# Second MLP of an encoder trunk: the first hidden unit's weight operands prepared during the output projection

## The chip, the cores and the metric

The kernel runs on one core of one Trainium2 chip (trn2). The metric is the device time of one execution in microseconds (us), as the median of several runs. The engines are named as in the profile: PE (TensorE, matmuls; PEld are its weight loads), DVE (VectorE), ACT (ScalarE), POOL (GpSimd) and SP (SyncE, whose queue issues all the DMAs that matter here).

## The reference, cut to what matters

Two layers (`DEPTH = 2`) on one sequence of 1024 rows of 1024 float32 values. Layer 0 mixes tokens with pooling, layer 1 with differential attention; after each mixer stands a gated MLP with 2816 hidden columns.

```python
for i in range(DEPTH):
    hn = _rms_norm(h, mix_norm[i])
    y = _pool_mixer(...) if i == 0 else _diff_attention(...)   # the latter ends in  o @ w_o
    h = h + y
    h = h + _conv_ffn(_rms_norm(h, ffn_norm[i]), ffn_w_up[i], ffn_conv_w[i], ffn_conv_b[i], ffn_w_down[i])
return _rms_norm(h, final_norm)

def _rms_norm(x, gain, eps=1e-6):
    y = x * lax.rsqrt(jnp.mean(x * x, axis=-1, keepdims=True) + eps)
    return y * gain

def _conv_ffn(x, w_up, conv_w, conv_b, w_down):
    g, u = jnp.split(x @ w_up, 2, axis=-1)
    gc = conv_b + sum(conv_w[j] * gp[:, j:j + s] for j in range(3))     # gp: g padded by one row
    return (jax.nn.gelu(gc, approximate=False) * u) @ w_down
```

## The kernel before

Each float32 factor of a matmul is kept as two parts, `hi` (rounded to the matmul's format, float32r) and `lo` (what is left), and each product is three matmuls: hi·hi, lo·hi and hi·lo. The up projection of the MLP is done by a scheme of Strassen's kind: for a block of 128 hidden columns (a *unit*; there are 22) the weights form four quarters, `u1`, `u2` (the two halves of the contraction, of the `u` columns) and `g1`, `g2` (of the `g` columns). Seven products of 12 matmuls each replace eight. Their weight operands are numbered 1 to 7: 1 is `u1`, 2 is `u2`, 4 is `g2`, and the others are sums: 5 is `g1+g2`, 6 is `g1+g2-u1`, 7 is `u1-g1`, 3 is `u2` minus operand 6. The row side has operands `x[1]` to `x[7]` with the same numbers: `x[1]`, `x[2]` come from rows 0 to 511, the others from sums of the upper and the lower 512 rows. A unit runs its products in the order 1, 6, 2, 7, 5, 4, 3.

`prep(j)` makes the weight operands of unit j from two loaded tiles `raw` (`ru` and `rg`, 512 KB each, `load(j)`): `parts` copies to `hi` on ACT (L379) and takes `lo = src - hi` (L380), `s_tile` makes a sum (L394). For j > 0 the sums and the `lo` are on POOL. For j = 0 they are on DVE, but for the `lo` of operands 1 and 2, which are on POOL.

The place of the change is the seam between the attention's output projection and this second MLP, at 1377 to 1478 us. The projection runs over eight row tiles of 128 rows, in the order `ORDER = (0, 4, 1, 5, 2, 6, 3, 7)`. For each tile (`wo_rest`):

- PE adds up 2 groups of 12 matmuls (`wo_acc`, L1251);
- DVE adds them to the residual `hs` (L175), ACT squares with a running sum (L176);
- the norm's factor is a chain of six small instructions of one column: `ss` (L188), `ms`, ACT's root `rt` (L190), `rt` (L192), `rs_p`, `rs_q`, `rs_r` (L194, L196, L198), all but `rt` on DVE;
- ACT scales to `xs` (L292), and PE transposes it by eight small matmuls into two PSUM tiles `tp` (L299), of which only two exist (`ps_dn`, two buffers), so that the second four transposes of a tile wait until ACT has read the first half of the tile before;
- for tiles 0 to 3, DVE takes `tp` into `xf` (L309). For tiles 4 to 7, ACT multiplies the first half by the gain in four instructions (L331, `b12`) and DVE does the second half (L309, `b22`), and then `combine` makes the sums of the two row halves (`t3`, `b12`, `b11`, `b21`: L340, L341, L342, L344) and the parts of `x[6]`, `x[7]`, `x[5]`, `x[4]`, `x[3]` (`put`: ACT L304, then DVE or POOL L305).

The profile leaves buffer numbers out of names: `t3` reads `t`, both `b12` and `b22` read `b`, `b11` and `b21` are halves of `xf`, `x[1]`, `x[2]`, `x[5]`, `x[3]` lie in `hnT_hi`/`hnT_lo`, and `x[6]`, `x[7]`, `x[4]` in tiles `x_hi`/`x_lo`.

A helper, `each_with_lag(ORDER, wo_rest, early)`, runs the combine of a tile after the first part of the next one, and calls `early()` once, after tile 1; `early` steps the generator `mlp`, which issues the loads of unit 0 and the first part of its prep. Outside of two hand ordered stretches (units 1 to 21 and the down projection) a list scheduler puts each engine's instructions in order, by its own estimate of their times; the order on each engine is then fixed, and each engine runs its list strictly in that order.

Pools that matter: `raw` (four buffers of 4 KB per partition, also used for `xf`), `s` (four buffers of 4 KB, of which a sum uses 2 KB), `wc` (16 weight parts), `u2`, `cm` and `wd` (free until unit 0 or 1 writes them). `w_combos(q)`, called in units 1, 3, 5 and so on, loads a 1 MB piece of the down weights into `wd` and makes four sums on DVE (L442 to L448).

Of the kernel before, what the change touches and what calls it, by code (L numbers as in the profile page):

```python
# [20 lines left out]
P = 128  # L21
# [3 lines left out]
NF = DFF // P  # L25
NT = S // P
NK = D // P
ORDER = (0, 4, 1, 5, 2, 6, 3, 7)
PLAN = ("...saq.bS..c.p", "st.aS.m.q.fb....F.c..")
PLAN7 = (".as.b....S.pqc.", "tmsaSqcb..f......F..")  # L30
# [59 lines left out]
def trunk_kernel(  # L90
# [133 lines left out]
    class Arena:  # L224


        def __init__(self, name):
            self.name = name
            self.s = None
            self.es, self.es_x, self.es_r, self.es_s, self.es_w = (ExitStack() for _ in range(5))  # L230

        def open(self):
# [22 lines left out]
        def open_up(self):  # L255
            self.es_r.close()
            if self.s is None:
                self.s = pool(self.es_s, "s", bufs=4, side="right")
            self.g = pool(self.es_r, "g", bufs=3, side="right")
            self.u2 = pool(self.es_r, "u2", bufs=2, side="right")  # L260
            self.cm = pool(self.es_r, "cm", side="right")
            self.wd = pool(self.es_r, "wd", side="right")
# [24 lines left out]
    def norm_to_x(layer, tt, ar, h_t, ss):  # L287
        x, G = ar.x, nc.gpsimd
        r = rstd(ss)
        with tc.high_priority(offset=20 if layer else 0):  # L290
            xs = ar.tile("gc", [P, D], F32, "xs")
            A.mul(xs, h_t, r)  # L292
            nc.sync.dma_start(h_dram[3 * layer][tt], h_t)
            cs = slice((tt % 4) * P, (tt % 4 + 1) * P)
            pts = []
            for q in range(2):
                pt = ar.tile("ps_dn", [P, 4, P], F32, "tp")
                for k in range(4):
                    PE.transpose(pt[:, k], xs[:, (4 * q + k) * P:(4 * q + k + 1) * P], ident)  # L299
                pts.append(pt)  # L300

        def put(i, src, eng):
            hi, lo = x[i]
            A.copy(hi[:, :, cs], src)  # L304
            eng.tensor_tensor(lo[:, :, cs], src, f32(hi[:, :, cs]), ALU.subtract)  # L305

        def gained(q, dst):
            gk = gcol[:, 2 + layer, 4 * q:4 * q + 4].unsqueeze(2).broadcast_to([P, 4, P])
            V.tensor_tensor(dst, pts[q], gk, ALU.mult)  # L309
            return dst  # L310

        q0, q1 = slice(0, 4), slice(4, 8)
        if tt < 4:
            xf = ar.xf[tt] = ar.tile("raw", [P, NK, P], F32, "xf")
            gained(0, xf[:, q0])
            gained(1, xf[:, q1])

            def combine():
                with tc.high_priority(offset=50):
                    combine2()  # L320

            def combine2():
                put(1, xf[:, q0], (V if layer else G))
                put(2, xf[:, q1], G)
        else:
            xf = ar.xf.pop(tt - 4)
            b11, b21 = xf[:, q0], xf[:, q1]
            b12, b22 = (ar.tile("s", [P, 2, 512], F32, n)[:, 0].rearrange("p (k f) -> p k f", f=P) if layer else
                        ar.tile("wc", [P, 4, P], F32, n) for n in ("b12", "b22"))
            for k in range(4):  # L330
                A.mul(b12[:, k], pts[0][:, k], gcol[:, 2 + layer, k:k + 1])  # L331
            gained(1, b22)

            def combine():
                with tc.high_priority(offset=20 if layer else 0):
                    combine2()

            def combine2():
                t3 = ar.tile("u2", [P, 4, P], F32, "t3")
                V.tensor_tensor(t3, b22, b12, ALU.subtract)  # L340
                V.tensor_tensor(b12, b12, b11, ALU.subtract)  # L341
                V.tensor_tensor(b11, t3, b11, ALU.add)  # L342
                put(6, b11, V)
                V.tensor_tensor(b21, b21, b11, ALU.subtract)  # L344
                put(7, t3, G)
                put(5, b12, V)
                put(4, b21, G)
                put(3, b22, G)

        return combine  # L350
# [12 lines left out]
    def ffn(layer, ar, tail, extra=None):  # L363
        G = nc.gpsimd
        wup, wdn, cv = w_up[layer], w_down[layer], convp[layer]
        raws, ws = {}, {}

        def load(j):
            if j >= NF:
                return  # L370
            raws.setdefault(j, [])
            for off in (DFF, 0):
                r = ar.tile("g" if layer == j == 0 else "raw", [P, NK, P], F32, "raw")
                nc.sync.dma_start(r, wup[:, off + j * P:off + (j + 1) * P].rearrange("(k p) f -> p k f", p=P))
                raws[j].append(r)

        def parts(src, eng=G):
            hi, lo = (ar.tile("wc", [P, 4, P], F32R, n) for n in ("w_hi", "w_lo"))
            A.copy(hi, src)  # L379
            eng.tensor_tensor(lo, src, f32(hi), ALU.subtract)  # L380
            return hi, lo

        def prep(j):
            if j >= NF:
                return
            w = ws.setdefault(j, {})
            ru, rg = raws.pop(j)
            u1, u2, g1, g2 = ru[:, 0:4], ru[:, 4:8], rg[:, 0:4], rg[:, 4:8]

            eng = (V, G)[j > 0]  # L390

            def s_tile(a, b, op):
                t = ar.tile("s", [P, 2, 512], F32, "s")[:, 0].rearrange("p (k f) -> p k f", f=P)
                eng.tensor_tensor(t, a, b, op)  # L394
# [314 lines left out]
            return ends[2:]  # L709

        load(0)
        first = prep(0)
        next(first)
        if layer:
            next(first)
        yield
        load(1)
        for _ in first:
            pass
# [16 lines left out]
    ar = Arena("a")  # L736
# [651 lines left out]
            ss = add_halves(hs, accs)  # L1388
        return norm_to_x(1, tt, ar, hs, ss)

    each_with_lag(ORDER, wo_rest, lambda: next(mlp))


    fin = []
# [53 lines left out]
```

## Time and profile before

| what | value |
|---|---|
| median of 3 runs | 2084.54 us (2083.7 to 2086.34) |
| profiled execution | 2089.84 us, span 2088.0 us |
| busy: PE, PEld | 2003.6 us (96%), 1665.6 us (80%) |
| busy: DVE, ACT, POOL | 1560.6 us (75%), 1024.4 us (49%), 895.3 us (43%) |
| mean granted PE clock | 0.983 |
| chain that ended last | PE 59%, DVE 5%, ACT 2%, DMA 2% |

Busy time is the sum of an engine's instructions in the span. A wait in brackets in a row is the idle time of the engine just before that instruction, and what ended it. All stages but the seam and the two ends keep PE busy without a pause.

### The profile page before, as it was taken

Reading aid. Unit: us, or ns where it says so; the run is one execution under the profiler, and the core shown is the slowest. Engines: PE = TensorE matmul, PEld = TensorE weight load, DVE = VectorE, ACT = ScalarE, POOL = GpSimd, SP = SyncE. Lnnn points to the kernel's source line nnn. Section 1 sums busy time; section 2 is a strip of 40 time slices with the busy share of each in tenths; the row PEclk is TensorE's granted clock in tenths of the full one; section 3 lists DMA queues with packets and bytes.
Section 4 is the critical chain, followed back from the end, with each engine's and each line's share of the span. In section 5 each row is a group of like instructions: output and inputs, shape, how many; then the busy total and the mean of one; then the engine's idle time right before and its main releaser. Section 6 shows DMA issues by size and latency. Waiting matters only on the chain.

```text
span 2088.0 us, 27647 instructions
## 1 busy us (share of the span) xinstructions
PE 2003.6 (96%) x9659; PEld 1665.6 (80%) x9659; DVE 1560.6 (75%) x2294; ACT 1024.4 (49%) x1838; POOL 895.3 (43%) x676
## 2 busy tenths in 40 slices
PE   5789999999999999999999998997999999999998
PEld 5768888888888877888888887875888888888886
DVE  6877777777665748899899888778667777775665
ACT  5743333333443645676667666456433333334443
POOL 4489999997000000101110110114999999930000
PEclk7889999999999999999999999999999999999999
DMA  4226445454876512122212115253345545458663
GB/s 153 99 70 198 141 154 184 132 177 151 334 239 221 207 56 66 48 75 61 61 46 77 54 35 197 101 172 118 121 160 167 172 149 179 142 191 334 201 211 132
DMA packets 221720, 301.90 MB, mean 145 GB/s; under 512 B 17852, under 2 KB 142092, under 8 KB 218764
## 3 DMA queue, kind: packets, MB, share of 16 engines
q1 hardware_dynamic: 221580, 300.13, 44.0%
q8 instruction: 76, 1.25, 0.2%
q14 instruction: 64, 0.52, 0.1%
HBM read 196.78 MB, written 90.70 MB: 138 GB/s over the span
## 4 chain that ended last, share of the span: by engine, by line
PE 59%; DVE 5%; ACT 2%; DMA 2%; issue 1%; SPq 1%; POOL 0%; ACTq 0%; DVEq 0%; POOLq 0%
PE dn L596 14%; PE up_b L422 8%; PE pj L1027 7%; PE up_c L422 5%; PE up_a L422 5%; PE sc L1113 5%; PE pj L1069 4%; PE po L1155 3%; PE aT L1144 3%; PE pj L1251 2%; DVE nm L1115 1%; DMA kf<-t 1%; ACT prob L1118 1%; DMA raw<-in_ffn_w_up_dram 0%; PE wo_acc L1251 0%
## 5 line engine op out<-in xcount | busy, mean ns | idle before, releaser
L1095 POOL TENSOR_TENSOR q_lo<-qt,q_hi 128x256 fp32r<-128x256 f32 x64 | 49.6, 776 | 683.4 <-ACT q_hi L1094 351.0
L380 POOL TENSOR_TENSOR w_lo<-s,w_hi 128x512 fp32r<-128x512 f32 x168 | 273.9, 1630 | 17.7 <-ACT w_hi L379 17.2
L596 PE MATMUL dn<-hnT_hi 128*128 128x512 f32 x560 | 218.3, 390 | 0.4 <-DVE hda L617 0.2
L596 PE MATMUL dn<-hnT_lo,hnT_hi 128*128 128x512 f32 x560 | 217.9, 389 | 0.0
L596 PE MATMUL dn<-hnT_hi,hnT_lo 128*128 128x512 f32 x560 | 217.9, 389 | 0.0
L422 PE MATMUL up_b<-x_hi,w_hi 128*128 128x512 f32 x528 | 207.2, 392 | 5.8 <-ACT x_hi L304 4.6
L422 PE MATMUL up_b<-x_lo,w_hi 128*128 128x512 f32 x528 | 206.4, 391 | 2.3 <-DVE x_lo L305 2.3
L380 POOL TENSOR_TENSOR w_lo<-raw,w_hi 128x512 fp32r<-128x512 f32 x130 | 195.1, 1501 | 30.0 <-ACT w_hi L379 26.5
L422 PE MATMUL up_b<-x_hi,w_lo 128*128 128x512 f32 x528 | 206.2, 391 | 0.0
L379 ACT CAST w_hi<-s 128x512 fp32r<-128x512 f32 x176 | 108.4, 616 | 179.1 <-PE up_b L422 87.3
L1115 DVE TENSOR_REDUCE nm<-sc 128x1 f32<-128x1024 f32 x128 | 155.8, 1217 | 15.7 <-PE sc L1113 15.0
L579 ACT CAST hnT_hi<-mst 128x1024 fp32r<-128x1024 f32 (+1 forms) x76 | 74.7, 983 | 164.7 <-PE dn L596 123.1
L1118 ACT ACTIVATE prob<-sc,nm 128x1024 f32<-128x1024 f32 x128 | 142.7, 1115 | 23.3 <-DVE nm L1115 11.6
L580 DVE TENSOR_TENSOR hnT_lo<-mst,hnT_hi 128x1024 fp32r<-128x1024 f32 (+1 forms) x76 | 86.5, 1138 | 90.1 <-ACT hnT_hi L579 90.1
L422 PE MATMUL up_a<-hnT_hi,w_hi 128*128 128x512 f32 x352 | 139.3, 396 | 1.4 <-ACT g L499 0.9
L422 PE MATMUL up_a<-hnT_lo,w_hi 128*128 128x512 f32 x352 | 138.8, 394 | 0.1
L422 PE MATMUL up_a<-hnT_hi,w_lo 128*128 128x512 f32 x352 | 138.5, 394 | 0.0
L394 POOL TENSOR_TENSOR s<-raw 128x512 f32<-128x512 f32 x84 | 133.1, 1584 | 10.3 <-DMA raw<-in_ffn_w_up_dram 4.1
L422 PE MATMUL up_c<-hnT_hi,w_lo 128*128 128x512 f32 x352 | 137.1, 389 | 0.3 <-DVE w_lo L380 0.3
L422 PE MATMUL up_c<-hnT_hi,w_hi 128*128 128x512 f32 x352 | 136.9, 389 | 0.0
L422 PE MATMUL up_c<-hnT_lo,w_hi 128*128 128x512 f32 x352 | 136.9, 389 | 0.0
L596 PEld LDWEIGHTS dn<-hnT_hi 128*128 128x128 f32 x560 | 105.1, 188 | 22.9 <-DVE hda L617 1.2
(304 smaller groups left out, 5433.3 us busy)
## 6 DMA issues: line engine op xcount, KB each, us to landing
raw<-in_ffn_w_up_dram SPq DMA_DIRECT2D x88, 512.0 KB, 4.3
mst<-m_dram SPq DMA_DIRECT2D x70, 512.0 KB, 6.2
wd<-in_ffn_w_down_dram SPq DMA_DIRECT2D x22, 1024.0 KB, 6.0
wd_dram<-wd SPq DMA_DIRECT2D x22, 1024.0 KB, 6.4
m_dram<-cm SPq DMA_DIRECT2D x80, 256.0 KB, 5.6
wst<-wd_dram SPq DMA_DIRECT2D x40, 512.0 KB, 4.8
m_dram<-gc SPq DMA_DIRECT2D x66, 256.0 KB, 6.3
wst<-in_ffn_w_down_dram SPq DMA_DIRECT2D x30, 512.0 KB, 7.2
```

What stands on the lines that cost most here:

```text
L379: A.copy(hi, src)
L380: eng.tensor_tensor(lo, src, f32(hi), ALU.subtract)
L394: eng.tensor_tensor(t, a, b, op)
L422: PE.matmul(acc, l[a][:, k], r[b][:, k], start=first and n == 0, stop=n == 11, skip_group_check=True)
L579: A.copy(h_, x)
L580: V.tensor_tensor(l_, x, f32(h_), ALU.subtract)
L596: PE.matmul(banks[t], l[:, q, cols], r[:, q], start=first and cnt == 0, stop=stop and cnt == 3 * n - 1, skip_group_check=True)
L1027: PE.matmul(acc, l[:, k % 2, h], r[:, k], start=(n == 0), stop=(n == 3 * NK - 1))
L1069: PE.matmul(acc, l[:, k % 4], r[:, k], start=(n == 0), stop=(n == 3 * NK - 1))
L1113: PE.matmul(sc[:, ns_], l[:, c], ks[:, c, ns_], start=(l is qhi), stop=(l is qlo))
L1115: V.tensor_reduce(nm, sc, AX.X, ALU.max, negate=True)
L1118: A.activation(soft[j, i][c], sc, AF.Exp, bias=nm, accum_out=sm[:, c, i:i + 1])
```

## The change

For layer 1 (`READY = (1,)`) a new generator `prep_first` makes all operands of unit 0, with every sum and every `lo` on POOL. The sums are written over the raw weights (`g2` becomes operand 5, `g1` operand 7, `u1` operand 6, `u2` operand 3). The operand tiles are put where space is free at that time: 7 and 5 in `cm`, 4 and 3 in `wd`, 1 and 6 in `s`, 2 in `wc`. `early` steps `mlp` twice: first operands 1 and 4, then the sums and operands 6, 7, 5; operands 2 and 3 follow after the last tile's code. The pool `s` of the second MLP has eight buffers of 2 KB in place of four of 4 KB. Layer 0 keeps `prep(0)`.

```diff
-            self.s = None
+            self.s, self.s_shape = None, [P, 2, 512]
...
-                self.s = pool(self.es_s, "s", bufs=4, side="right")
+                self.s = pool(self.es_s, "s", bufs=8, side="right")
+                self.s_shape = [P, 1, 512]
...
+        def prep_first():
+            w = ws.setdefault(0, {})
+            ru, rg = raws.pop(0)
+            u1, u2, g1, g2 = ru[:, 0:4], ru[:, 4:8], rg[:, 0:4], rg[:, 4:8]
+            room = {}
+            (room[7], room[5]), (room[4], room[3]) = pairs("cm"), pairs("wd")
+            if layer:
+                room[1], room[6] = pairs("s") + pairs("s")
...
+            w[1] = parts(u1, G, room[1])
...
+            w[4] = parts(g2, G, room[4])
+            yield
+            for o, x, y, op, i in ((g2, g1, g2, ALU.add, 5), (g1, u1, g1, ALU.subtract, 7),
+                                   (u1, g2, u1, ALU.subtract, 6)):
+                G.tensor_tensor(o, x, y, op)
+                if i == 6:
+                    w[6] = parts(o, G, room[6])
+            for i, o in ((7, g1), (5, g2)):
+                w[i] = parts(o, G, room[i])
+            if layer:
+                yield
+                w[2] = parts(u2, G)
+            G.tensor_tensor(u2, u2, u1, ALU.subtract)
+            w[3] = parts(u2, G, room[3])
...
-        first = prep(0)
+        first = prep_first() if layer in READY else prep(0)
         next(first)
-        if layer:
+        if layer and layer not in READY:
             next(first)
         yield
+        if layer in READY:
+            next(first, None)
+            yield
...
-    each_with_lag(ORDER, wo_rest, lambda: next(mlp))
+    each_with_lag(ORDER, wo_rest, lambda: next(mlp) or next(mlp))
```

The scheduler gives three engines another order at the seam. Line numbers of the changed kernel are higher (L379 and L380 become L390 and L391, L292 becomes L294, L331 becomes L333, L304 and L305 become L306 and L307, L394 becomes L434); the new sums are L412 and L420. Parts of operands 7, 5, 4 and 3 are named `w_hl`.

ACT before, from the scaling of tile 5 to that of tile 2 (the `b` are the gain multiplications of tile 5):

```order
L292 ACTIVATE xs<-hs,rs_r 128x1024
L176 ACTIVATE wo_acc,ss<-hs 128x512
L331 ACTIVATE b_13795<-tp,gcol 128x128
L190 ACTIVATE rt<-ss,eps 128x1
L331 ACTIVATE b_13795<-tp,gcol 128x128 x3
L304 CAST hnT_hi_69<-b_13796 128x4x128
L304 CAST x_hi<-t_13867 128x4x128
L176 ACTIVATE wo_acc,ss<-hs 128x512
L292 ACTIVATE xs<-hs,rs_r 128x1024
```

and now, from the scaling of tile 5 to the gain multiplications of tile 5 and the two squares of tile 6:

```order
L294 ACTIVATE xs<-hs,rs_r 128x1024
L390 CAST w_hi<-raw 128x512
L177 ACTIVATE wo_acc,ss<-hs 128x512
L390 CAST w_hl<-raw 128x512
L191 ACTIVATE rt<-ss,eps 128x1
L294 ACTIVATE xs<-hs,rs_r 128x1024
L390 CAST w_hl<-raw 128x512
L390 CAST w_hi<-raw 128x512
L390 CAST w_hl<-raw 128x512
L333 ACTIVATE b_13798<-tp,gcol 128x128 x4
L306 CAST hnT_hi_69<-b_13799 128x4x128
L177 ACTIVATE wo_acc,ss<-hs 128x512 x2
```

Tile 5's multiplications moved from ahead of tile 2's scaling to behind it and behind the casts of operands 7, 6 and 5, which read POOL's sums.

POOL before, from the parts of tile 1 to those of tile 6 (two of unit 0's operand parts stand between them):

```order
L305 TENSOR_TENSOR hnT_lo_68<-xf,hnT_hi_67 128x4x128
L305 TENSOR_TENSOR hnT_lo_70<-b_13796,hnT_hi_69 128x4x128
L305 TENSOR_TENSOR x_lo<-t_13867,x_hi 128x4x128
L305 TENSOR_TENSOR x_lo<-xf,x_hi 128x4x128
L305 TENSOR_TENSOR hnT_lo_68<-xf,hnT_hi_67 128x4x128
L380 TENSOR_TENSOR w_lo<-raw,w_hi 128x512 x2
L305 TENSOR_TENSOR x_lo<-t_14012,x_hi 128x4x128
```

and now, from the parts of tile 1 to those of tile 5:

```order
L307 TENSOR_TENSOR hnT_lo_68<-xf,hnT_hi_67 128x4x128
L391 TENSOR_TENSOR w_lo<-raw,w_hi 128x512
L391 TENSOR_TENSOR w_hl<-raw,w_hl 128x512
L412 TENSOR_TENSOR raw<-raw 128x512 x3
L391 TENSOR_TENSOR w_hl<-raw,w_hl 128x512
L391 TENSOR_TENSOR w_lo<-raw,w_hi 128x512
L391 TENSOR_TENSOR w_hl<-raw,w_hl 128x512
L307 TENSOR_TENSOR hnT_lo_70<-b_13799,hnT_hi_69 128x4x128
L307 TENSOR_TENSOR x_lo<-t_13870,x_hi 128x4x128
```

Eight instructions of unit 0's prep now stand in a row ahead of the parts of tile 5.

DVE before, from the combine of tile 7 to unit 0's first sum `u` (L510):

```order
L340 TENSOR_TENSOR t_14096<-b_14086,b_14085 128x512
L341 TENSOR_TENSOR b_14085<-b_14085,xf 128x512
L342 TENSOR_TENSOR xf<-t_14096,xf 128x512
L394 TENSOR_TENSOR s<-raw 128x512
L344 TENSOR_TENSOR xf<-xf 128x512
L305 TENSOR_TENSOR x_lo<-xf,x_hi 128x4x128
L305 TENSOR_TENSOR hnT_lo_70<-b_14085,hnT_hi_69 128x4x128
L380 TENSOR_TENSOR w_lo<-s,w_hi 128x512
L394 TENSOR_TENSOR s<-raw,s 128x512
L380 TENSOR_TENSOR w_lo<-s,w_hi 128x512
L380 TENSOR_TENSOR w_lo<-raw,w_hi 128x512
L510 TENSOR_TENSOR u_14167<-up_b,g 128x512
```

and now:

```order
L342 TENSOR_TENSOR t_14099<-b_14089,b_14088 128x512
L343 TENSOR_TENSOR b_14088<-b_14088,xf 128x512
L344 TENSOR_TENSOR xf<-t_14099,xf 128x512
L346 TENSOR_TENSOR xf<-xf 128x512
L307 TENSOR_TENSOR hnT_lo_70<-b_14088,hnT_hi_69 128x4x128
L307 TENSOR_TENSOR x_lo<-xf,x_hi 128x4x128
L550 TENSOR_TENSOR u_14157<-up_b,g 128x512
```

Unit 0's prep has left DVE's list here, and `x_lo` (of `x[6]`) now stands behind `hnT_lo` (of `x[5]`).

PE keeps its order up to tile 3's transposes; in unit 0 the products 2 and 6 are interleaved in another way. On SP's queue, the load of the first 1 MB piece of the down weights stood in the attention stage; it now stands behind the loads of units 1, 2 and 3, and waits for unit 0's last matmul, which reads operand 3 in `wd`.

More of the change, by code (lines that the diff above doesn't have):

```diff
@@ L27 @@
 NK = D // P
+READY = (1,)
 ORDER = (0, 4, 1, 5, 2, 6, 3, 7)
@@ L327, in norm_to_x @@
             b11, b21 = xf[:, q0], xf[:, q1]
-            b12, b22 = (ar.tile("s", [P, 2, 512], F32, n)[:, 0].rearrange("p (k f) -> p k f", f=P) if layer else
+            b12, b22 = (ar.tile("s", ar.s_shape, F32, n)[:, 0].rearrange("p (k f) -> p k f", f=P) if layer else
                         ar.tile("wc", [P, 4, P], F32, n) for n in ("b12", "b22"))
@@ L375, in load, with pairs, parts @@
                 raws[j].append(r)
-        def parts(src, eng=G):
-            hi, lo = (ar.tile("wc", [P, 4, P], F32R, n) for n in ("w_hi", "w_lo"))
+        def pairs(where):
+            if where in ("cm", "wd"):
+                t = ar.tile(where, [P, 2, 2, 4, P], F32R, "w_hl")
+                return [(t[:, i, 0], t[:, i, 1]) for i in range(2)]
+            if where == "g":
+                t = ar.tile(where, [P, 2, 4, P], F32R, "w_hl")
+                return [(t[:, 0], t[:, 1])]
+            return [tuple(ar.tile(where, [P, 4, P], F32R, n) for n in ("w_hi", "w_lo"))]
+        def parts(src, eng=G, into=None):
+            hi, lo = into or pairs("wc")[0]
             A.copy(hi, src)
@@ L381, in parts @@
             return hi, lo
+        def prep_first():
[6 more added lines that the diff above has]
+                room[1], room[6] = pairs("s") + pairs("s")
+            else:
+                room[1], room[2] = pairs("wc") + pairs("wc")
+                room[6], = pairs("g")
+            w[1] = parts(u1, G, room[1])
+            if not layer:
+                w[2] = parts(u2, G, room[2])
+            w[4] = parts(g2, G, room[4])
[12 more added lines that the diff above has]
+            w[3] = parts(u2, G, room[3])
         def prep(j):
@@ L392, in s_tile @@
             def s_tile(a, b, op):
-                t = ar.tile("s", [P, 2, 512], F32, "s")[:, 0].rearrange("p (k f) -> p k f", f=P)
+                t = ar.tile("s", ar.s_shape, F32, "s")[:, 0].rearrange("p (k f) -> p k f", f=P)
                 eng.tensor_tensor(t, a, b, op)
```

## The prediction

> **What bounds the kernel now.** I read the page's busy shares first (PE 96%), then cut the stretch around the change into windows to see where PE pauses at all. Columns: stretch, length, busy time and instructions of PE, PEld, DVE, ACT and POOL, granted PE clock, DMA share, GB/s.
>
> ```profile
> 1377.00:1420.00 43.00, 39.29 (x195) 31.59 (x194) 33.32 (x77) 28.34 (x60) 9.93 (x7) 1.00 0.55 183
> 1420.00:1448.00 28.00, 19.89 (x81) 15.41 (x80) 22.22 (x41) 16.75 (x35) 11.57 (x8) 0.82 0.28 94
> 1448.00:1478.00 30.00, 26.77 (x115) 20.44 (x113) 19.80 (x23) 16.26 (x28) 21.45 (x15) 1.00 0.25 71
> 1478.00:1880.00 402.00, 401.76 (x1773) 332.52 (x1773) 295.42 (x283) 144.88 (x209) 351.31 (x220) 1.00 0.51 163
> ```
>
> From 1478 to 1880 us PE is busy 401.76 of 402: the eight sum buffers can give nothing there, since nobody waits for a sum. In the 101 us before, PE idles 3.7, 8.1 and 3.2 us, 15 in all. That is all the change can win. Next the waits of PE from 1377 to 1478 us (total us, times, longest), and PE's timeline at the places where a wait ends last:
>
> ```profile
> PE tp L299 <- ACT xs L292: 9.8, 4, 4.8
> PE up_b L422 <- DVE x_lo L305: 1.5, 1, 1.5
> ...
> 1419.06 1.09 PE L299 MATMUL tp<-ident,xs 128*128 128x128 f32 x8
> 1428.76 1.10 PE L299 MATMUL tp<-ident,xs 128*128 128x128 f32 x8 [2.68 <-ACT xs L292]
> 1439.64 1.97 PE L299 MATMUL tp<-ident,xs 128*128 128x128 f32 x8 [4.77 <-ACT xs L292]
> 1447.07 1.46 PE L299 MATMUL tp<-ident,xs 128*128 128x128 f32 x8
> 1455.49 0.50 PE L422 MATMUL up_b<-x_lo,w_hi 128*128 128x512 f32 x1 [1.50 <-DVE x_lo L305]
> 1469.86 0.39 PE L422 MATMUL up_a<-hnT_hi,w_hi 128*128 128x512 f32 x1
> ```
>
> These are the transposes of tiles 2, 6, 3 and 7, the first use of `x_lo` of `x[6]`, and the start of unit 1. PE's two large waits (2.68, 4.77) are for the norm chains of tiles 6 and 3, and a chain is slow where DVE meets POOL:
>
> ```profile
> 1398.97 1.29 POOL L305 TENSOR_TENSOR hnT_lo<-b,hnT_hi 128x512 fp32r<-128x512 f32 x1 [4.24 <-ACT hnT_hi L304]
> 1400.23 1.74 POOL L305 TENSOR_TENSOR x_lo<-t,x_hi 128x512 fp32r<-128x512 f32 x1
> 1399.03 1.79 DVE L341 TENSOR_TENSOR b<-b,xf 128x512 f32<-128x512 f32 x1
> 1400.74 0.68 DVE L175 TENSOR_TENSOR hs<-wo_acc,hs 128x512 f32<-128x512 f32 x1
> ```
>
> DVE's `b` starts behind POOL's and takes 1.79 us where such an instruction takes 0.68. POOL's next one then takes 1.74 where the free one took 1.29. So a DVE instruction with two inputs in SBUF stands until POOL's running one has ended (1.29 + about 0.56), and POOL stands in turn. When both have a backlog, one DVE instruction of this kind gets through per POOL instruction, one pair each 1.85 us.
>
> **The change, part by part, as shifts of PE's times.** *Tile 2.* ACT's list now holds unit 0's casts ahead of tile 5's multiplications.
>
> ```profile
> 1407.04 1.50 SPq L374 DMA_DIRECT2D raw<-in_ffn_w_up_dram  x2
> DMA to landing us min/median/max: 3.7/3.9/4.2
> 1411.44 1.15 ACT L292 ACTIVATE xs<-hs,rs_r 128x1024 f32<-128x1024 f32 x1
> 1413.46 0.60 ACT L176 ACTIVATE wo_acc<-hs 128x512 f32<-128x512 f32 x1 [0.86 <-DVE hs L175]
> 1417.85 1.15 ACT L292 ACTIVATE xs<-hs,rs_r 128x1024 f32<-128x1024 f32 x1
> 1428.61 0.60 ACT L379 CAST w_hi<-raw 128x512 fp32r<-128x512 f32 x1
> 1429.51 1.14 ACT L331 ACTIVATE b<-tp,gcol 128x128 f32<-128x128 f32 x4 [0.30 <-PE tp L299]
> ```
>
> The raw weights land by 1407.04 + 1.50 + 3.9 = 1412.4, just before tile 5's scaling ends (1412.59), so the first cast ends at 1413.2 and operand 4's, behind the square, at 1414.7. POOL, idle there, does the two `lo` by about 1416.0 and three sums at 1.29 by 1419.9, say 1420.1 with one port wait. ACT has scaled tile 2 by 1419.0; cast 7 ends at 1419.6, cast 6 waits for the third sum and ends at 1420.7, cast 5 at 1421.2, and the four multiplications (1.14) at 1422.35. PE's second four transposes of tile 2 need the `tp` that these free: they start at 1422.4 instead of 1419.6, 2.8 us late. That is covered by the wait ahead of tile 6's transposes: PE was ready for them at 1428.76 − 2.68 = 1426.1, and is now at 1428.9. Without that cover it would cost 2.8.
>
> *Tile 6's chain.* Its factor (`rs_r`) now queues on DVE behind the late combine of tile 5, with POOL busy throughout. Tile 5's first sum `t` waits for POOL's `lo` of operand 6 (three instructions behind the sums' 1420.1, two being `lo` of 7 and 6: 1422.65) and ends at 1423.2. Until `rs_r`, POOL has four more to run: the `lo` of operand 5, `hnT_lo` and `x_lo` of tile 5, `hnT_lo` of tile 2. At 1.85 each that is 7.4, so `rs_r` ends at 1430.65, the scaling (1.15) at 1431.8, and the transposes start at about 1431.85: **+3.1** on 1428.76. From below, if only one-column instructions (0.16) meet POOL, 4 × 1.45 = 5.8, so +1.5. From above, one period more, +4.9. I take the middle, since the list there holds large and small instructions by turns, as in the rows at 1399.
>
> *Tile 6's transposes to tile 3's.* Before: 1439.64 − 1428.76 = 10.88.
>
> ```profile
> 1430.51 3.00 POOL L380 TENSOR_TENSOR w_lo<-raw,w_hi 128x512 fp32r<-128x512 f32 x2 [3.45 <-issue]
> 1427.30 0.16 DVE L198 SCALAR_TENSOR_TENSOR rs_r<-rs_q,rt 128x1 f32<-128x1 f32 x1
> 1432.28 1.25 DVE L188 TENSOR_TENSOR ss<-ss 128x1 f32<-128x1 f32 x1
> 1435.45 1.22 DVE L196 SCALAR_TENSOR_TENSOR rs_q<-rs_p,rt 128x1 f32<-128x1 f32 x1
> 1437.19 1.21 DVE L198 SCALAR_TENSOR_TENSOR rs_r<-rs_q,rt 128x1 f32<-128x1 f32 x1
> 1438.44 1.15 ACT L292 ACTIVATE xs<-hs,rs_r 128x1024 f32<-128x1024 f32 x1 [1.89 <-DVE rs_r L198]
> ```
>
> Three of tile 3's small instructions already pay about 1.05 each against the free 0.16. Before, two `w_lo` (3.00) stood in POOL's list here; now there are three: `lo` of 2, operand 3's sum, `lo` of 3. One more is one more period if DVE has a backlog: **+1.8** (bounds: −1.1, a wait less, since DVE's own `w_lo` of operand 5 has left that list; +3.7, two periods). Nearest is the row at 1432.28, where the chain met exactly these `w_lo`. In place of that wait, tile 3's transposes are late next, at 1439.64 + 3.1 + 1.8 = 1444.5.
>
> *Tile 3's transposes to `x_lo`.* Before: 1455.49 − 1439.64 = 15.85.
>
> ```profile
> 1439.53 1.28 DVE L175 TENSOR_TENSOR hs<-wo_acc,hs 128x512 f32<-128x512 f32 x2
> 1444.08 0.63 PE L422 MATMUL up_a<-hnT_hi,w_hi 128*128 128x512 f32 x1
> 1452.47 1.75 DVE L394 TENSOR_TENSOR s<-raw 128x512 f32<-128x512 f32 x1
> L380 DVE TENSOR_TENSOR w_lo<-s,w_hi 128x512 fp32r<-128x512 f32 x4 | 3.8, 953 | 0.0
> ```
>
> Tile 7's residual adds ended at 1440.81, 1.17 after the transposes began. PE reaches them later now while DVE does not depend on it, so they should end about 0.1 after: −1.0. The sum at 1452.47 (1.75, with its port wait) has left DVE's list; `hnT_lo` (about 0.6) has moved ahead of `x_lo`: −1.15. One of ten cold up matmuls fewer (0.63 by the record, the steps being 0.43) stands ahead of tile 7's transposes: −0.3. Together **−2.5** (bounds: −3.5, with operand `lo` off DVE too; 0, if tile 7's chain is held by POOL as tile 3's was). The four `w_lo` of 3.8 us that also leave DVE cost nothing before, because PE had the products 1 and 2 to do beside them, so I give them nothing.
>
> *Unit 0's rest.* From the use of `x_lo` to unit 1: 1469.86 − 1455.49 = 14.37 before, for 59 matmuls with some short waits; in the new order 62 follow, at 401.76 / 1773 = 0.227 each, by the last window above, 14.05: **−0.3**.
>
> *The load into `wd`.* It now waits for unit 0's last matmul, about 1472 by the old clock. Its price is a landing:
>
> ```profile
> wd<-in_ffn_w_down_dram SPq DMA_DIRECT2D x22, 1024.0 KB, 6.0
> 1478.29 1.17 DVE L442 TENSOR_TENSOR wd<-wd 128x512 f32<-128x512 f32 x1
> ```
>
> 1472.2 + 6.0 = 1478.2, just when DVE first read it, and PE needs nothing of it; behind L442 on DVE stands L517, wanted by PE 60 matmuls (13.7 us) into unit 1, at about 1485.9. I give it 0; with the cover gone it is a rival below. SP's raw loads for unit 1 go out behind tile 7's store, about 1445.7, and land about 1450, before ACT wants them: 0.
>
> Sum: +3.1 + 1.8 − 2.5 − 0.3 = **+2.1**. The profiled execution (2089.84, span 2088.0 and 1.84 around it) would go to 2091.9; it stands 5.3 above the median 2084.54, so the median goes to 2086.6. A measurement of this kernel tells about 0.2% (4.2 us) from no change, so this is a forecast of no measurable change.
>
> POOL's price rests on the free row of 1.29 us. The Trainium skill ("GPSIMD Engine Reference", section 3.1 "Elementwise — side-by-side cycle accounting") gives about 2.6 cycles per element for a sum of two inputs, by its 1.2 GHz an estimate of 1.11 us; with four POOL periods of 0.18 less the sum would be +1.4. The row of 1.29 decides, as it has the issue in it.
>
> **The rivals.** *Faster: POOL and DVE do not collide.* If POOL's eight instructions are done before tile 5's combine, tile 6's transposes come at PE's own 1428.9 (+0.1), and tile 3's chain loses its three port waits (1.25 + 1.22 + 1.21 − 3 × 0.16 = 3.2): 0.1 − 3.2 − 2.5 − 0.3 = −5.9, 2078.6. It decides if tile 6's `rs_r` ends by about 1427.7. For it: POOL has long pauses (9.93 busy of 43). Against: the first parts can't begin before 1413.2.
>
> *Slower: POOL at its crowded pace.* This row of the page has the mean of 84 sums in the units:
>
> ```profile
> L394 POOL TENSOR_TENSOR s<-raw 128x512 f32<-128x512 f32 x84 | 133.1, 1584 | 10.3 <-DMA raw<-in_ffn_w_up_dram 4.1
> ```
>
> At 1.58 instead of 1.29, tile 2's transposes slip 1.2 more and five periods 0.3 each: +1.2 + 1.5 + 2.1 = +4.8, 2089.3. It decides when the sums meet DVE's chains of tiles 2 and 5 at each step.
>
> *Slower: every added POOL instruction stops DVE for its length.* Nine are added (four sums, five `lo`); with all on the path, 9 × 1.29 = 11.6, less 2.5: +9.1, 2093.6. The rows of 1.2 speak for the price; against it, DVE is busy only 33 of 43 us where most of them run. It decides if tile 6's transposes come after 1436. The Trainium skill ("SBUF — State Buffer", section "Who interferes with whom") states this: a DVE instruction with two SBUF inputs and a GpSimd instruction that reads SBUF exclude each other, and the later one waits for the whole of the other. The trace agrees on the wait (1.21 against 0.16).
>
> *Slower: the load into `wd` lands late.* At twice 6.0, DVE's four sums end after 1485.9 and PE stands about 1.9: 2.1 + 1.9 = +4.0, 2088.5.
>
> **How the numbers follow.** Forecast 0.55, with a range of its own of 2082 to 2091 (terms at their lower or upper bounds, not all together). No collision 0.20, crowded POOL 0.14, full stops 0.07, late load 0.04. Faster by over 0.2%: 0.17, of the first rival. Slower: 0.08 of the forecast, 0.09 of crowded POOL, 0.07, and 0.02 of the late load, 0.26. The rest, 0.57, is the same. The range goes from the first rival's 2078.6, rounded to 2078.5, to 2092, which leaves out the full stops and some of that rival's lower edge.
>
> **What would show it.** Right: in PE's timeline tile 2's second transposes at about 1422.4 waiting for ACT's `b`, tile 6's at about 1431.8 and tile 3's at 1444.5, both for `xs`; `rs_q` and `rs_r` of 1.2 on DVE near POOL's parts; no L394 sum on DVE before `x_lo`; `x_lo` used at about 1457.5. Wrong: `rs_r` of tile 6 at 0.16 with PE waiting under 1 us; casts on ACT that wait for POOL beyond 1424; L442 waiting for the load; or any pause of PE after 1478.

## The result, and the profile after

The changed kernel takes 2139.18 us (median of 4 runs, 2132.24 to 2142.59), the kernel before 2084.12 us (2082.08 to 2086.34). The ratio is 1.026, with a 95% interval of 1.0236 to 1.0284: 55 us slower, where 2.1 were forecast. The profiled execution is the fastest of the four (2132.24, span 2130.5), 50.2 above the fastest run of before. The medians differ by 5 us more than the stages below, which are read from that one execution; where the slower runs lose them stays open.

The first thing to read is the page's fourth part, the chain that ended last, by engine. POOL had 0% of it before:

```profile
PE 70%; POOL 10%; DVE 8%; DMA 5%; ACT 3%; issue 3%; SPq 1%; POOLq 0%; ACTq 0%; DVEq 0%
```

The same windows as before the change (stretch, length, busy time and instructions of PE, PEld, DVE, ACT, POOL, granted PE clock, DMA share, GB/s) show where:

```profile
1377.00:1420.00 43.00, 37.70 (x177) 30.50 (x177) 30.41 (x64) 29.30 (x63) 20.80 (x16) 0.96 0.48 160
1420.00:1448.00 28.00, 18.42 (x74) 13.92 (x73) 22.10 (x37) 17.63 (x37) 16.95 (x12) 0.79 0.33 94
1448.00:1478.00 30.00, 27.83 (x107) 21.26 (x105) 14.78 (x13) 10.39 (x15) 29.22 (x22) 0.85 0.29 88
1478.00:1880.00 402.00, 374.44 (x1586) 301.37 (x1585) 236.28 (x248) 128.34 (x189) 308.23 (x202) 0.98 0.42 137
```

The last one is the stretch in which PE never paused before (401.76 of 402, 1773 matmuls). Now it does 1586 in the same time, at a clock of 0.98. The waits of PE and of POOL in the units (1480 to 1940 us; total us, times, longest) name the two links of the chain:

```profile
PE up_c L462 <- POOL w_lo L391: 21.8, 14, 2.5
PE up_a L462 <- POOL w_lo L391: 5.0, 9, 0.6
...
POOL s L434 <- DMA raw<-in_ffn_w_up_dram: 90.3, 18, 5.9
```

PE waits for POOL's `w_lo`, and POOL waits for the raw weights, 18 times, 5.0 us each. Before, POOL waited for no load there. One such wait in full, from the timelines of POOL and of SP's queue:

```profile
1504.41 3.00 POOL L391 TENSOR_TENSOR w_lo<-s,w_hi 128x512 fp32r<-128x512 f32 x2
1507.37 1.30 POOL L391 TENSOR_TENSOR w_lo<-raw,w_hi 128x512 fp32r<-128x512 f32 x1
1513.88 1.29 POOL L434 TENSOR_TENSOR s<-raw 128x512 f32<-128x512 f32 x1 [5.22 <-DMA raw<-in_ffn_w_up_dram]
...
1508.69 0.38 SPq L376 DMA_DIRECT2D raw<-in_ffn_w_up_dram  x1
```

The `w_lo` of 1507.37 ends at 1508.67. It is the last reader of a raw buffer. SP issues the load into that buffer 0.02 us later, and the very next instruction on POOL is the first reader of what it brings: 5.2 us from the release to the use, with nothing between. Before, the same round trip stood here:

```profile
1735.23 1.30 POOL L380 TENSOR_TENSOR w_lo<-raw,w_hi 128x512 fp32r<-128x512 f32 x1
1736.99 1.90 POOL L380 TENSOR_TENSOR w_lo<-s,w_hi 128x512 fp32r<-128x512 f32 x1 [0.46 <-ACT w_hi L379]
1738.97 2.16 POOL L394 TENSOR_TENSOR s<-raw,s 128x512 f32<-128x512 f32 x1
1742.00 1.30 POOL L380 TENSOR_TENSOR w_lo<-raw,w_hi 128x512 fp32r<-128x512 f32 x1 [0.88 <-ACT w_hi L379]
1743.26 1.75 POOL L380 TENSOR_TENSOR w_lo<-s,w_hi 128x512 fp32r<-128x512 f32 x1
1745.09 1.61 POOL L394 TENSOR_TENSOR s<-raw 128x512 f32<-128x512 f32 x1
...
1736.56 0.38 SPq L374 DMA_DIRECT2D raw<-in_ffn_w_up_dram  x1
```

The release is at 1736.53 and the first use at 1745.09: four instructions stand between, 8.6 us, and the load is hidden under them.

What moved is POOL's order in the units. "Hand ordered" holds there for PE, DVE and ACT; POOL's and SP's lists are the scheduler's in units 1 to 21 as well. Here are two units of its list, written as one letter for each instruction: S a sum, l a `w_lo` that reads a sum, r a `w_lo` that reads a raw tile (r\* is operand 4's, the last reader of the `g` tile; S\* is `g1+g2`, the first reader of its next content, two units on):

```
before   S* r  l  S  l  S  r* l  S  r  l  S* r  l  S  l  S  r* l  S  r  l
after    S* S  S  l  S  r  l  r  l  l  r* S* S  S  l  S  r  l  r  l  l  r*
```

With four sum buffers a sum had to wait until an earlier one had been read; that held the sums back among the `w_lo`, as the list of before shows. With eight, the scheduler puts the sums a whole unit ahead, the `w_lo` of a unit then come last, and r\* ends next to S\*. I count the *distance* from r\* to the S\* that needs the buffer again: 5 before, 1 after.

By stages, from PE's timeline (first matmul of the projection's tiles, transposes of tiles 6 and 3, first use of `x_lo`, first matmul of unit 1, first of the down projection, end of the span):

| stage | before | after | difference | forecast |
|---|---|---|---|---|
| projection to tile 6's transposes | 51.68 | 54.52 | +2.84 | +3.1 |
| to tile 3's | 10.88 | 11.95 | +1.07 | +1.8 |
| to `x_lo` | 15.85 | 18.30 | +2.45 | −2.5 |
| to unit 1 | 14.37 | 15.94 | +1.57 | −0.3 |
| units 1 to 21 | 400.37 | 442.74 | +42.37 | 0 |
| down projection | 217.79 | 217.79 | 0.00 | 0 |

The sum is +50.3. The spans differ by 42.4, since the projection starts 7.87 us earlier in the profile of after (1369.21 against 1377.08). That is no gain of the change: over the kept profiles this start lies between 1367.5 and 1377.6, with and without the new preparation. The ends of the stages that the prediction does not show, of before and then of after:

```profile
1377.08 0.40 PE L1251 MATMUL wo_acc<-wo_l,hnT_hi 128*128 128x512 f32 x1
1870.23 0.39 PE L596 MATMUL dn<-hnT_hi 128*128 128x512 f32 x1
...
1369.21 0.40 PE L1294 MATMUL wo_acc<-wo_l,hnT_hi 128*128 128x512 f32 x1
1469.92 0.39 PE L462 MATMUL up_a<-hnT_hi,w_hi 128*128 128x512 f32 x1
1912.66 0.39 PE L636 MATMUL dn<-hnT_hi 128*128 128x512 f32 x1
```

### The profile page after: what moved, and what is told of

It is laid out like the page before. It is cut to its first block, busy times and chain, and to the rows that moved or that the text cites. A ratio compares the mean times of both kernels' runs of the same rounds, so it can differ in the third digit from the quotient of the medians.

```text
span 2130.5 us, 27689 instructions
## 1 busy us (share of the span) xinstructions
PE 2022.1 (95%) x9659; PEld 1671.3 (78%) x9659; DVE 1530.5 (72%) x2285; ACT 1024.3 (48%) x1838; POOL 891.5 (42%) x685
## 4 chain that ended last, share of the span: by engine, by line
PE 70%; POOL 10%; DVE 8%; DMA 5%; ACT 3%; issue 3%; SPq 1%; POOLq 0%; ACTq 0%; DVEq 0%
PE dn L636 18%; PE up_b L462 11%; PE up_c L462 8%; PE up_a L462 7%; POOL w_lo L391 7%; PE pj L1070 6%; PE sc L1156 4%; PE pj L1112 4%; PE po L1198 3%; DMA raw<-in_ffn_w_up_dram 3%; POOL s L434 3%; PE aT L1187 2%; PE pj L1294 2%; PE pp L891 1%; PE pl L871 1%
## 5 line engine op out<-in xcount | busy, mean ns | idle before, releaser
L391 POOL TENSOR_TENSOR w_lo<-s,w_hi 128x512 fp32r<-128x512 f32 x168 | 263.4, 1573 | 10.8 <-ACT w_hi L390 10.5
L391 POOL TENSOR_TENSOR w_lo<-raw,w_hi 128x512 fp32r<-128x512 f32 x131 | 202.3, 1545 | 20.4 <-ACT w_hi L390 20.4
L390 ACT CAST w_hi<-s 128x512 fp32r<-128x512 f32 x172 | 105.9, 616 | 173.3 <-PE up_b L462 89.8
L434 POOL TENSOR_TENSOR s<-raw 128x512 f32<-128x512 f32 x84 | 127.0, 1512 | 95.9 <-DMA raw<-in_ffn_w_up_dram 92.8
L390 ACT CAST w_hi<-raw 128x512 fp32r<-128x512 f32 x132 | 81.5, 618 | 85.2 <-PE up_c L462 80.2
```

## The experiments

Theory A: the eight buffers reorder POOL's list, the distance falls from 5 to 1, and a load's round trip of 5 to 6 us is exposed on POOL in each unit. Rivals: the new preparation of unit 0 does it (B), or the number of buffers by itself (A2). Theory S is for the seam: a POOL instruction in a norm chain or a combine costs DVE's chain about 1.1 us wherever it stands. "Units" below is the time of units 1 to 21, "seam" the time from the projection's first matmul to unit 1, both from one profile; before, they are 400.37 and 92.78. The time that is given first is the median, and the ratio is to the kernel before, run beside it. The edits of the first five kernels and of the last two are to the changed kernel, the others to the kernel before, with their main lines shown.

**Eight sum buffers alone.**

```diff
-READY = (1,)
+READY = ()
-    each_with_lag(ORDER, wo_rest, lambda: next(mlp) or next(mlp))
+    each_with_lag(ORDER, wo_rest, lambda: next(mlp))
```

> The kernel before with nothing changed but the sum buffers: eight of 2 KB in place of four of 4 KB; unit 0 is prepared as before. Theory A (the eight buffers let the list scheduler put the sums of a unit ahead of the lo parts of the unit before, so that the raw weights of that unit are released only after its last lo part, and the next load is exposed on POOL): the loss of the units comes back in full without the new preparation, some 40 us: 2120 to 2132, POOL waiting about 4.7 us for raw in each unit, and no loss at the seam. Rival B (the new preparation is to blame, by the load into wd that now stands behind the raw loads on SP's queue): about 2084, no wait of POOL for raw.

2135.49 us, ratio 1.0251 (1.0229 to 1.0273). Units 450.7, seam 95.46. POOL's waits:

```profile
POOL s L434 <- DMA raw<-in_ffn_w_up_dram: 90.2, 18, 6.0
```

So the whole loss of the units comes back without the new preparation, and B falls. The median is 3.5 above the expected range. The expected "no loss at the seam" was wrong: 2.7 us are lost there, all behind tile 7's transposes (they come 69.98 after the projection's start, 69.99 before the change). With free buffers, a sum of unit 1 comes forward on POOL into tile 7's combine, and on DVE a `w_lo` of unit 0 (1.75 us) now stands ahead of `x_lo`.

**Four sum buffers of 2 KB with the new preparation.**

```diff
-                self.s = pool(self.es_s, "s", bufs=8, side="right")
+                self.s = pool(self.es_s, "s", bufs=4, side="right")
-                room[1], room[6] = pairs("s") + pairs("s")
+                room[1], room[6] = pairs("wc") + pairs("wc")
```

> The changed kernel with four sum buffers of 2 KB; the parts of operands 1 and 6 of unit 0 lie in wc, since four buffers have no room for them. Theory A: the units run without a pause of PE, as before (400.4 us for units 1 to 21), and only the seam's loss of some 8 us stays: 2089 to 2094. Rival B: the units stay slow, 2130 to 2140.

2093.77 us, 1.0053 (1.0036 to 1.007). Units 400.77, seam 103.96. POOL waits for ACT only, and for no load:

```profile
POOL w_lo L391 <- ACT w_hi L390: 36.7, 38, 8.4
...
1500.00:1850.00 350.00, 350.00 (x1546) 289.91 (x1545) 266.48 (x241) 123.17 (x183) 320.08 (x202) 1.00 0.50 161
```

PE is busy without a pause again (350 of 350), as A expected. The seam is worse than in the changed kernel (+11.2 against +7.9): with other rooms the scheduler made another order there, in which all eight transposes of tile 2 wait 4.48 us for `xs`.

**Eight buffers, POOL in the order of the code.**

```diff
+UNIT_ENGINES = ENGINES | {mybir.EngineType.Pool}
-        with tc.manual_schedule(engines=ENGINES):
+        with tc.manual_schedule(engines=UNIT_ENGINES):
```

> The changed kernel with its eight buffers, but POOL's list in units 1 to 21 in the order of the code instead of the scheduler's. Theory A (the order costs, not the buffers): 2089 to 2096, the units near 400 us. Rival A2 (eight buffers cost by themselves, by where they lie or by what they collide with): 2130 to 2140. Rival B: 2130 to 2140.

2105.4 us, 1.0095 (1.0071 to 1.0119). In this order the distance from r\* to S\* is 15, and the same count at the `u` tile, the tighter one here, is 13. POOL waits for no load, and the units take 405.04. Without the order the eight buffers do not bring the loss of 42, and A2 falls. The median is 9 above the expected range. The profiled execution (2097.29, the lowest) agrees with its stages: +8.9 at the seam, +4.7 in the units, where each unit but the first takes 19.2 to 19.3 instead of 19.04. PE's own rows show next to no wait there, but its weight loads (PEld) do, once in each of 20 units (1480 to 1860 us, then one case from the timeline):

```profile
PEld up_b L463 <- DVE u L551: 7.5, 20, 1.1
...
1517.66 1.29 POOL L392 TENSOR_TENSOR w_lo<-raw,w_hi 128x512 fp32r<-128x512 f32 x1 [0.58 <-ACT w_hi L391]
1517.72 1.78 DVE L516 TENSOR_TENSOR gc<-u,gc 128x512 f32<-128x512 f32 x1
1519.42 0.68 DVE L551 TENSOR_TENSOR u<-up_b,g 128x512 f32<-128x512 f32 x1
1520.15 0.19 PEld L463 LDWEIGHTS up_b<-x_hi,w_hi 128*128 128x128 f32 x1 [0.35 <-DVE u L551]
```

DVE's `u` comes late because two DVE instructions ahead of it are longer here: at the mean `gc` of L516 takes 1.78 (1.51 before) and the `gc` of L577 2.28 (1.53 before). In the case shown, L516 starts 0.06 behind a `w_lo` of POOL. So this order trades the wait for the load against meetings of POOL and DVE inside the units. Why the other runs are 8 higher stays open.

**Six and five buffers, old preparation.** The kernel of the first experiment with fewer buffers; the distances are 1 and 2.

```diff
-                self.s = pool(self.es_s, "s", bufs=8, side="right")
+                self.s = pool(self.es_s, "s", bufs=6, side="right")     # and bufs=5
```

> The kernel before with six sum buffers of 2 KB. POOL's order then is again one sum and one or two lo parts by turns, with the sums about half a unit ahead. Theory A: the raw weights are released about 1.5 sums later than before, still ahead of the next load's need: within 5 us of 2084, a few short waits of POOL for raw at most. A theory by which each further buffer costs a share would give 2100 or more.

> The kernel before with five sum buffers of 2 KB. Counted in POOL's list, from the last lo part that reads a raw buffer to the first sum that reads its next content, the distance at the tighter of the two buffers is 5 in the kernel before, 1 with six and with eight, and 2 here. Theory A (refined: a load's round trip of some 6 us, from the release to the data, must fit into the instructions between): one instruction of about 1.6 us covers part of it, POOL idles 3 to 4.5 us in each unit, its 16.1 us of work become 19.4 to 20.3 a unit against PE's 19.04: 2090 to 2108, between before and the 2136 of six buffers. A theory that any buffer more than four brings the full loss: 2130 or more. A theory that five are harmless: 2082 to 2086.

Six: 2136.42 us, 1.0247 (1.023 to 1.0265), units 449.17. Theory A as I had it then (the sums being ahead by more or less) said "within 5 us" and was wrong. Its list shows what I had not counted: r\* stands next to S\* again, although sums and `w_lo` come by turns. That is where the distance as the quantity comes from. Five: 2110.52 us, 1.0117 (1.0098 to 1.0136), units 426.71, which is between, 2.5 above the expected range. POOL's waits of six, then of five:

```profile
POOL s L434 <- DMA raw<-in_ffn_w_up_dram: 70.3, 15, 6.2
```

```profile
POOL s L434 <- DMA raw<-in_ffn_w_up_dram: 53.5, 17, 4.6
```

The mean wait falls from 4.7 at distance 1 to 3.1 at distance 2, which is about the length of the one POOL instruction that now stands between. Eight buffers (450.7) are hardly worse than six (449.2), so it is not a cost by buffer.

**Each raw load issued twice.** The kernel before, four buffers, distance 5:

```diff
                 nc.sync.dma_start(r, wup[:, off + j * P:off + (j + 1) * P].rearrange(...))
+                if layer and j > 0:
+                    nc.sync.dma_start(r, wup[:, off + j * P:off + (j + 1) * P].rearrange(...))
```

> The kernel before, where each raw load of units 1 to 21 is issued twice into the same buffer (the second one repeats the first); buffers and POOL's order in the units as before, distance 5. If the second transfer waits for the first, the round trip is some 10.5 us and four instructions (6.4 us) no longer cover it. Theory A: POOL waits for raw about 4 us in each unit and the units take 20 to 20.5 us each: 2100 to 2115, with nothing else changed. If the cause of the slow units is not the round trip but something that more sum buffers do, 2083 to 2088. If the two transfers run side by side, also about 2084 to 2090, and the run tells nothing.

2120.62 us, 1.0163 (1.0147 to 1.0179), units 435.62. POOL waits for raw and PE for POOL, with buffers and order as before:

```profile
POOL s L396 <- DMA raw<-in_ffn_w_up_dram: 82.9, 19, 6.6
...
PE up_a L424 <- POOL w_lo L382: 21.3, 10, 3.8
```

The second load of a pair goes out about a landing later (4.3 us at the median) than the first. For one `g` tile the first went out at 1539.94, right behind r\*, the second at 1544.33, and S\* started at 1551.08, 11 us after the release:

```profile
1544.08 1.30 POOL L382 TENSOR_TENSOR w_lo<-s,w_hi 128x512 fp32r<-128x512 f32 x1
1551.08 1.26 POOL L396 TENSOR_TENSOR s<-raw 128x512 f32<-128x512 f32 x1 [5.70 <-DMA raw<-in_ffn_w_up_dram]
```

The waits are 4.4 us a unit, near the expected 4; the time is 5.6 above the range. POOL's own work is about the 16.1 us a unit that I had counted with (293.98 us busy from 1500 to 1880, at 20.74 a unit). Unit 1 takes 24.4, and the others take 20.6 at the mean, close to the expected 20 to 20.5. So a longer round trip, with the buffers and POOL's order as before, makes the same slow units.

**The seam: early parts of operands 1 and 2 alone, and operand 3 on POOL.** The kernel before with

```diff
...
+            room = pairs() if j == 0 and layer else (None, None)     # two pairs in "wd"
-            w[1] = parts(u1, G)
+            w[1] = parts(u1, G, room[0])
             if j == 0:
-                w[2] = parts(u2, G)
+                w[2] = parts(u2, G, room[1])
```

and, in the second one, operand 3 on POOL (`G`) instead of DVE:

```diff
-            w[3] = parts(s_tile(u2, s2, ALU.subtract), eng)
+            e3 = G
...
+            e3.tensor_tensor(t3s, u2, s2, ALU.subtract)     # t3s: a tile of "s"
+            w[3] = parts(t3s, e3)
```

> The kernel before with one part of the change: only the parts of operands 1 and 2 of unit 0 are laid into wd instead of wc, so that ACT's two casts and POOL's two lo parts are done before tile 5's combine, when POOL is idle, and not inside tile 3's norm chain. Sums, their lo parts on DVE, and the four sum buffers of 4 KB stay. Theory S (the seam is set by the meetings of DVE and POOL in the norm chains): tile 3's chain loses its three waits of about 1.05, 3 us: 2080 to 2082.5, the transposes of tile 3 about 59.5 us after the projection's first matmul instead of 62.56. Rival: the freed place is filled by other parts, 2083 to 2086.

> As the run with early parts of operands 1 and 2, and operand 3's sum and lo part of unit 0 on POOL instead of DVE, behind tile 7's parts. Theory S: the sum of 1.75 us leaves the way to x_lo: 1 to 2 us less than that run, 2078.5 to 2081.5. Rival: operand 3's POOL instructions push unit 1's parts back or meet DVE in tile 7's combine: as fast as that run or slower.

2087.02 us, 1.0002 (0.9992 to 1.0013), seam 92.97; and 2088.28 us, 1.0008 (0.9997 to 1.0019), seam 93.22. No gain in either. PE's transposes of tiles 2, 6 and 3 in the first, with the meeting on DVE and POOL, and behind the last dots one row of DVE in the second:

```profile
1422.59 1.09 PE L299 MATMUL tp<-ident,xs 128*128 128x128 f32 x8 [2.70 <-ACT xs L292]
1429.86 1.09 PE L299 MATMUL tp<-ident,xs 128*128 128x128 f32 x8 [1.16 <-ACT xs L292]
1440.01 1.09 PE L299 MATMUL tp<-ident,xs 128*128 128x128 f32 x8 [3.81 <-ACT xs L292]
...
1413.70 1.49 DVE L398 TENSOR_TENSOR s<-raw 128x512 f32<-128x512 f32 x1
1415.22 1.66 DVE L398 TENSOR_TENSOR s<-s,raw 128x512 f32<-128x512 f32 x1
1413.35 2.98 POOL L384 TENSOR_TENSOR w_hl<-raw,w_hl 128x512 fp32r<-128x512 f32 x2 [1.79 <-ACT w_hl L383]
...
1447.86 1.76 DVE L398 TENSOR_TENSOR s<-raw 128x512 f32<-128x512 f32 x1
```

Tile 3's wait fell from 4.77 to 3.81, but POOL's two `lo` parts now meet DVE's two sums (1.49 and 1.66, where they took 0.69 each before), and tile 2 got a wait of 2.70 that it did not have. The rival held: the meetings only moved. The second run does not test its theory. The sum of 1.75 us on the way to `x_lo` reads two `raw` tiles (`s<-raw`), so it is operand 7's, not operand 3's (`s<-raw,s`); it still stands there, 1.76 us long.

**The whole change with the distance intact.** The parts of operands 1 and 6 in a pool of their own, four sum buffers:

```diff
-                self.s = pool(self.es_s, "s", bufs=8, side="right")
+                self.s = pool(self.es_s, "s", bufs=4, side="right")
+                self.first = pool(self.es_s, "first", bufs=4, side="right")
-                room[1], room[6] = pairs("s") + pairs("s")
+                room[1], room[6] = pairs("first") + pairs("first")
```

and, in a second one, one step after tile 1 and one after tile 2:

```diff
-            if tt == 1 and early is not None:
+            if tt in (1, 2) and early is not None:
-    each_with_lag(ORDER, wo_rest, lambda: next(mlp) or next(mlp))
+    each_with_lag(ORDER, wo_rest, lambda: next(mlp))
```

> The changed kernel with its seam left as it is: the parts of operands 1 and 6 of unit 0 in a pool of their own of four buffers of 2 KB, the sums in four of 2 KB (together as many bytes as before). POOL's list in the units is then that of the kernel before, distance 5. Theory A: units 1 to 21 in 400.4 to 401 us; what is left is the seam's own loss, 4 to 8 us (tile 6's transposes +2.8 and tile 3's +3.9 against the projection's first matmul, as in the changed kernel): 2088 to 2094. Rival: the new preparation costs in the units as well, over 2096.

> As the run with two pools, but the sums and the parts of operands 6, 7, 5 are issued one tile later in the code. The scheduler then leaves the three sums where they were and puts the four lo parts behind them between POOL's parts of tiles 5, 2 and 6, and tile 5's multiplications ahead of the casts on ACT. Theory S (a POOL instruction in a norm chain costs the chain about 1.1 us wherever it stands): tile 2's wait of 2.9 for ACT is gone, tile 6's transposes come 1 to 2 us earlier than in that run, tile 3's not; the seam is 1 to 3 us shorter: 2086 to 2092. Rival: the collisions only move on, as long as that run or longer.

2095.79 us, 1.0049 (1.0035 to 1.0064), units 400.81, seam 101.61; and 2092.79 us, 1.0034 (1.0021 to 1.0046), units 400.82, seam 100.84. The units are whole in both. The medians are 1.8 and 0.8 above their ranges. The first one's seam loses 8.8: this is what the new preparation itself costs, in the order that the scheduler gives it here (tile 2's transposes wait for `xs`, not for `b` as in the changed kernel). Stepping later shortened the seam by 0.8, not by 1 to 3; tile 6's transposes did not come earlier (56.7 after the projection's start, 56.5 in the first), and tile 2's wait is as long in both:

```profile
1425.89 1.97 PE L302 MATMUL tp<-ident,xs 128*128 128x128 f32 x8 [4.75 <-ACT xs L295]
```

```profile
1422.03 1.97 PE L302 MATMUL tp<-ident,xs 128*128 128x128 f32 x8 [4.88 <-ACT xs L295]
```

Theory S holds for the price of a meeting, and failed as a guide to gains: in the run with early parts and in the late one, a meeting that was taken away came back at another tile. No version here beats the kernel before.

## Why the prediction was wrong

**The step that failed** is its first reading: "the eight sum buffers can give nothing there, since nobody waits for a sum". That was right as far as it goes, and it was taken to mean that they could cost nothing either. A pool's size is also an input of the scheduler, which on POOL and SP is at work in the units too. The order listing of the changed kernel, read beyond the seam, shows S\* behind r\*; the row to weigh against it was the load's landing, 4.3 us at the median over the kernel (3.9 for unit 0's), against one instruction of 1.3 to 1.6. The sum looked for no term outside the seam: 0 forecast, +42.4 measured, of which PE's waits for `w_lo` are 26.8. Of the rest about 7.5 are steps of 0.43 in place of 0.23 from one matmul to the next, which PE's timeline shows behind these waits (the granted clock of the last window is 0.98). About 7 more stand in no row as a wait, but at the same places: a row counts a wait only from the end of the matmul before, 0.39 after its start, though the next would start 0.23 after it, and the step behind a wait is 0.34. None of the rivals had this mechanism, though the prediction named its sign ("any pause of PE after 1478"). The nearest, "POOL at its crowded pace", took the units' mean of 1584 ns for the seam and left the units themselves alone.

**The terms at the seam**, from PE's timeline of after and, behind the dots, DVE's and POOL's:

```profile
1414.56 0.66 PE L301 MATMUL tp<-ident,xs 128*128 128x128 f32 x4 [2.92 <-ACT b L333]
1423.73 1.09 PE L301 MATMUL tp<-ident,xs 128*128 128x128 f32 x8 [0.96 <-ACT xs L294]
1435.68 1.97 PE L301 MATMUL tp<-ident,xs 128*128 128x128 f32 x8 [5.84 <-ACT xs L294]
1442.67 1.32 PE L301 MATMUL tp<-ident,xs 128*128 128x128 f32 x8
1453.98 0.79 PE L462 MATMUL up_b<-x_lo,w_hi 128*128 128x512 f32 x1 [1.90 <-DVE x_lo L307]
...
1445.55 1.64 DVE L343 TENSOR_TENSOR b<-b,xf 128x512 f32<-128x512 f32 x1
1450.49 1.77 DVE L307 TENSOR_TENSOR hnT_lo<-b,hnT_hi 128x512 fp32r<-128x512 f32 x1
1452.18 1.75 DVE L307 TENSOR_TENSOR x_lo<-xf,x_hi 128x512 fp32r<-128x512 f32 x1
...
1449.97 1.74 POOL L434 TENSOR_TENSOR s<-s,raw 128x512 f32<-128x512 f32 x1
1451.66 1.71 POOL L434 TENSOR_TENSOR s<-raw 128x512 f32<-128x512 f32 x1
```

- Tile 2: as forecast. PE's second four transposes wait for ACT's `b`, 2.92 us (2.8 forecast), and the wait of tile 6, now 0.96 where it was 2.68, covers part of it.
- Tile 6's chain: +2.84 against +3.1. The mechanism is right; POOL's four instructions take 1.74, 1.73, 1.29 and 1.50, so 1.85 a meeting was a little dear. That the number is so close is in part luck: behind the wait for `b` PE's steps are 0.43 for about 3 us, and PE itself reaches these transposes at 1422.77, 1.9 later against the projection's start than they ran before, where the prediction had 0.1.
- Tile 3's chain: +1.07 against +1.8. Mechanism and sign right.
- Tile 3 to `x_lo`: −2.5 forecast, +2.45 measured. Up to tile 7's transposes it is −0.44 (6.99 against 7.43), where −1.3 were forecast: that is the one matmul fewer, a step of 0.43. The −1.0 for tile 7's adds is not there, as PE comes to these transposes from its matmuls without a wait in both. Behind them it fails: the sum of 1.75 did leave DVE, but five DVE instructions in a row take 1.58 to 1.77 instead of 0.68. POOL runs a `w_lo` of unit 1 (at 1445.32), tile 7's own two parts and two sums of unit 1 beside them; before, only tile 7's parts were there. Eight buffers alone lose about as much at this place (+2.3 between tile 7's transposes and `x_lo`), but by other rows, as said at that run. "What is late next" was not asked of POOL's list here.
- Unit 0's rest: −0.3 forecast, +1.57 measured. The term took its step, 0.227, from a window with a granted clock of 1.00. In the window from 1448 to 1478 the clock is now 0.85 (1.00 before), and at `x_lo` the steps are 0.43 until they return to 0.23:

```profile
1455.00 0.63 PE L462 MATMUL up_b<-x_hi,w_hi 128*128 128x512 f32 x1
1456.71 0.49 PE L462 MATMUL up_b<-x_lo,w_hi 128*128 128x512 f32 x1
1457.03 0.39 PE L462 MATMUL up_b<-x_hi,w_lo 128*128 128x512 f32 x1
```

- The load into `wd`: right. It went out at 1470.11 and DVE read it at 1478.87 without holding PE. In the runs with the new preparation and distance 5 the units take 400.8, 0.4 above before.
- The price of a meeting. By the Trainium skill ("SBUF — State Buffer", section "Who interferes with whom") the later of the two stands until the other's instruction has ended. The rows above agree: 1.7 us for an instruction of 0.68 while POOL's run 1.7 each. The rival of nine full stops on the path, +9.1, gives about the seam's own loss in the last two runs, 8.1 and 8.8 (11.2 in the one with the parts in `wc`). Its sign was not met, though: tile 6's transposes were to come after 1436, 7 us late, and come at +4.8 and +5.1 there.

## What to carry to other kernels

A ring of buffers is covered by what the consumer has to do between the last read of a buffer and the first read of its next content, not by the number of buffers. Count this distance in the consumer's own list whenever a neighbouring pool grows, since more buffers can let a scheduler run one kind of work ahead and shorten it: here a distance of 5, 2 and 1 instructions of some 1.6 us gave 400, 427 and 443 to 451 us for the same units. And where two engines hold each other up, as DVE and POOL did in the rows above, work that is moved to the idle one pays where both are needed, so the places where they meet are what to count, not the idle time.

## What the runs showed of the hardware that was not expected

POOL's free instruction of 128x512 takes 1.29 us, but in a stretch where DVE has two-input work of its own the two run in step: 1.7 for each POOL and 1.6 to 1.8 for each DVE instruction (rows above), so neither engine keeps its own pace. And PE can lose time without a row of PE that shows a wait: in the order of the code (third experiment) it lost 0.2 us a unit, and only the rows of its weight loads name DVE.
